# Finer steps for the decays that run between the tiles of v and the gate

## The chip, the cores and the metric

The kernel runs on 1 core of one Trainium2 chip. The metric is the device time of one execution in microseconds (us), median of several runs. All products are made in float32 precision from three products of split operands (high by high, high by low, low by high).

## The reference

One encoder block for 2048 tokens of width 1024. The first layer mixes a short convolution (512 channels) and a bidirectional gated linear attention of 4 heads (keys of 64, values of 128). Only the second part bears on the change:

```python
h = rms_norm(x, mix_norm)
z = h @ w_in                     # conv B, C, u; q, k, v, g; two low-rank gates
la_f = log_sigmoid(lr_f @ w_af + b_af) / 16      # decays, forward
la_b = log_sigmoid(lr_b @ w_ab + b_ab) / 16      # decays, backward
# per direction, in chunks: b = cumsum(la); q * exp(b), k * exp(-b),
# states carried over the chunks, o = (masked q k^T) v + q S
o = fwd + bwd - diag
y_gla = rms_norm(o, gla_norm) * silu(g)
x = x + concat([y_conv, y_gla]) @ w_out
# then cross-attention into 256 memory tokens, an MLP with squared ReLU, a final norm
```

## The kernel before, in words

The block is staged over the two halves of 1024 tokens. For each half, the operand of the norm is prepared, queries and keys are projected (`qk`), then the low-rank gates with the first half of the columns of g (`lr_g`), then the remaining columns of g and v (`vg`), and for the first half the convolution (`conv`). The weights come through `load_w` or `load_st`: a load into a `raw` buffer (L131 in `load_w`) and a split into a high part (a cast on ACT, L117) and a low part (a subtraction on DVE, L118). A product of split operands is `mm3`, L145 to L147.

`vg` works through three groups of columns, each 256 wide: one of g, two of v. In a group it makes eight token tiles of 128 x 256, each a chain of 24 matmuls into one of the four PS banks, so there are 24 tiles. `vg_store` evicts each: for g a Silu on ACT (L251), for v a copy on DVE (L249); then a store into the DRAM buffer zg or zv (L253). Behind each tile, `vg` takes one step of the generator `meanwhile`.

In the second half `meanwhile` is `decays()`, which makes the decays of heads 0 and 1 beside the tiles. For each head `gla_decay` has four steps of one small product with two evictions (L386 to L388), a step with two exponentials (L390), a step with two logarithms (L392), and then the part that the change touches, once for each half hf of the tokens:

- `sums(hf)`: on DVE a subtraction (L397), four running sums (L400), two small copies of the chunk's middle and end (L405, L406) and a subtraction (L407);
- `apply(hf)`: on ACT the exponentials for keys and queries (L411, L414); for keys and then queries, two blocks each: two DMAs from zk or zq on SP (L420) and a product on DVE (L422).

A last step makes the decay factors between chunks (L432 to L435). First come the four product steps of head 0, then those of head 1, then the rest of head 0, then the rest of head 1. Steps left over when the 24 tiles are done run behind them.

This stretch is in a block in which the instructions of PE, ACT and DVE keep the order in which they are written; the planner may put instructions from outside the block between them. The order on SP, which issues all DMAs, and on POOL, and everything behind the block, is laid out by the planner from its own estimates, and is then fixed.

Behind the block come the states of head 0: `gla_states`, with transposed keys (`keys`, L457, copied by ACT in L459), loads of v from zv (`load_v`, L440), products of the two (L465 in `upd`), their eviction (L469) and the `scan` over the chunks on DVE (L474). Then, head by head, `gla_out` (`attn` L485 to L489, `outp` L496 to L506, `fin` L512 to L515) beside the next head's states, and behind it the decays of head h + 2 through the same `gla_decay`, with no tile between its steps. The convolution of the second half (`conv(1, ...)`) is written behind all that, and the planner fills PE's waits with its products.

Of the kernel before, what the change touches and what calls it, by code (L numbers as in the profile page):

```python
# [30 lines left out]
def block_kernel(ctx, tc, x, mem, wm, wv, wlg, wlog, wout, wxk, wxv, wxqT, wxo, wup, wdn,  # L31
# [9 lines left out]
    def A4(dt=F32, shape=(P, 1024)):  # L41
        return big.tile(list(shape), dt, tag="a", name="a4", bufs=NA)

    def G4(dt=F32, shape=(P, 1024)):
        return big.tile(list(shape), dt, tag="g", name="g4", bufs=NG)
# [13 lines left out]
    def GT(dt=F32, shape=(P, 512)):  # L59
        return big.tile(list(shape), dt, tag="gt", name="gt", bufs=8)  # L60
# [4 lines left out]
    def GS(n, dt=F32):  # L65
        return big.tile([P, 16], dt, tag="gs", name="gs", bufs=9)[:, :n]
# [4 lines left out]
    def PG(shape=(P, 512)):  # L71
        return psp.tile(list(shape), F32, tag="pg", name="pg", bufs=4)
# [38 lines left out]
    def in_order(first, then):  # L111
        tc.add_manual_dep(then.ins, first.ins.name,
                          mybir.DependencyInfo(mybir.DependencyClass.NoSync, mybir.DependencyReason.DATA),
                          reason="one table set at a time")
# [28 lines left out]
    def mm3(ps, L, R, first, last):  # L143
        (lh, ll), (rh, rl) = L, R
        nc.tensor.matmul(ps, lh, rh, start=first, stop=False)  # L145
        nc.tensor.matmul(ps, lh, rl, start=False, stop=False)  # L146
        mark["pe"] = nc.tensor.matmul(ps, ll, rh, start=False, stop=last)  # L147
# [226 lines left out]
    def gla_decay(h, res):  # L374

        pr, r0 = h // 2, (h % 2) * 64
        hs = slice(h * P, (h + 1) * P)
        Q, K = [G4(), G4()], [G4(), G4()]
        pm, pe, de = GS(16), GS(16), GS(16)
        res.append((Q, K, de))  # L380

        for hf in range(2):
            for bi in range(2):
                ps = PG()
                sl = slice(bi * TB, (bi + 1) * TB)
                mm3(ps, (wlh[:, hs], wll[:, hs]), (lr[hf][0][:, sl], lr[hf][1][:, sl]), True, True)  # L386
                nc.scalar.activation(K[hf][:, sl], ps, AF.Abs)
                nc.vector.tensor_scalar_min(Q[hf][:, sl], ps, 0.0)  # L388
                yield
        exps = [nc.scalar.activation(K[hf], K[hf], AF.Exp, scale=-1.0) for hf in range(2)]  # L390
        yield
        lns = [nc.scalar.activation(K[hf], K[hf], AF.Ln, bias=1.0) for hf in range(2)]  # L392
        in_order(exps[1], lns[0])
        yield

        def sums(hf):
            nc.vector.tensor_tensor(out=K[hf], in0=Q[hf], in1=K[hf], op=ALU.subtract)  # L397
            for i in range(4):
                sl = slice(i * 256, (i + 1) * 256)
                nc.vector.tensor_tensor_scan(out=Q[hf][:, sl], data0=reset, data1=K[hf][:, sl], initial=0.0,  # L400
                                             op0=ALU.mult, op1=ALU.add)

            pv = Q[hf].rearrange("p (c t) -> p c t", t=P)
            m8 = pm[:, 8 * hf:8 * hf + 8].unsqueeze(2)
            nc.vector.tensor_copy(m8, pv[:, :, 63:64])  # L405
            nc.vector.tensor_copy(pe[:, 8 * hf:8 * hf + 8].unsqueeze(2), pv[:, :, 127:128])  # L406
            nc.vector.tensor_tensor(out=pv[:, :, 0:64], in0=pv[:, :, 0:64], in1=m8.broadcast_to([P, 8, 64]),  # L407
                                    op=ALU.subtract)

        def apply(hf):  # L410
            e = nc.scalar.activation(K[hf], Q[hf], AF.Exp, scale=nsgn)  # L411
            if hf == 0:
                in_order(lns[1], e)
            nc.scalar.activation(Q[hf], Q[hf], AF.Exp, scale=sgn)  # L414
            for T, z in ((K[hf], zk), (Q[hf], zq)):
                for bi in range(2):
                    r = GT()
                    c0 = hf * 1024 + bi * TB
                    for o in (0, 64):
                        nc.sync.dma_start(r[o:o + 64], z[pr][r0:r0 + 64, c0:c0 + TB])  # L420
                    sl = slice(bi * TB, (bi + 1) * TB)
                    nc.vector.tensor_tensor(out=T[:, sl], in0=T[:, sl], in1=r, op=ALU.mult)  # L422

        sums(0)
        yield
        apply(0)
        sums(1)
        yield
        apply(1)
        yield  # L430

        nc.vector.memset(de, 0.0)  # L432
        nc.vector.tensor_tensor(out=de[0:64, 1:16], in0=pe[0:64, 0:15], in1=pm[0:64, 1:16], op=ALU.add)
        nc.vector.tensor_tensor(out=de[64:128, 0:15], in0=pe[64:128, 0:15], in1=pm[64:128, 1:16], op=ALU.add)
        nc.scalar.activation(de, de, AF.Exp, scale=1.0 / 16.0)  # L435
        yield
# [396 lines left out]
    def decays():  # L833
        gens = [gla_decay(h, dec) for h in (0, 1)]
        for g in gens:
            for _ in range(4):
                next(g)
                yield
        for g in gens:
            for _ in g:  # L840
                yield
# [15 lines left out]
    for h in range(H):  # L857
        attn, outp, fin = gla_out(h, *dec[h][:2], St)
        if h + 1 < H:
            St, keys, upd, scan = gla_states(h + 1, *dec[h + 1])  # L860
        for j in range(6):
            if j < 4:
                attn(j)
                if h + 1 < H:
                    keys(j)
            if 0 < j < 5:
                outp(j - 1)
                if h + 1 < H:
                    upd(j - 1)
            if j > 1:  # L870
                fin(j - 2)
        if h + 1 < H:
            scan()
        if h + 2 < H:
            for _ in gla_decay(h + 2, dec):
                pass
# [362 lines left out]
    sums = [A4(F32, (P, 2, TB)) for _ in range(4)]  # L1239
# [172 lines left out]
```

## Time and profile before

| | |
|---|---|
| runs | 2677.62 us median of 3 (2676.23 to 2678.01) |
| profiled execution | 2673.82 us; its span, first to last instruction, 2672.0 us |
| mean granted clock of TensorE | 0.988 |
| PE, DVE, ACT, POOL busy | 97%, 61%, 35%, 10% of the span |
| the 24 tiles of the second half with their decays | about 482 to 564 us of the span |
| of them the 16 tiles of v | from 510.5 us on |
| linear attention and the convolution behind it | about 564 to 870 us |

The profile is of one execution. Times within it are us from the start of the span. PE is the matmul side of TensorE and PEld its weight loads, which overlap the matmuls; SPq is the queue in which SP issues DMAs. A row of a timeline gives start, length, engine, line, operation, what is written and read, shapes and count; in brackets stands how long the engine had been idle and what ended that. A row of waits gives who waited for whom, the total, the number and the longest. The chain of waits goes back from the last instruction to what released each step.

### The profile page before, as it was taken

The numbers are of one execution on the slowest core, as the hardware profiler recorded it, in microseconds if no ns is written. First come the engines' busy times: TensorE is split into PE (matmuls) and PEld (weight loads), VectorE is DVE, ScalarE is ACT, GpSimd is POOL, SyncE is SP. The second block draws the span as 40 slices with busy tenths as digits, with TensorE's granted clock in tenths as the row PEclk, the third lists the DMA queues.
The fourth block names the chain that finished last, engine by engine and source line by source line (L and its number), as shares of the span: only waits on it lengthen the run. The fifth ranks groups of instructions, "written<-read, shape, count | busy, mean of one in ns | idle before, by whom it ended". The sixth has DMA issues, their size and how long they took to land.

```text
span 2672.0 us, 34688 instructions
## 1 busy us (share of the span) xinstructions
PE 2580.3 (97%) x13560; PEld 2199.2 (82%) x13560; DVE 1627.1 (61%) x2502; ACT 934.0 (35%) x1432; POOL 259.9 (10%) x178
## 2 busy tenths in 40 slices
PE   7999999989989999999999999999999999999998
PEld 7898888877777787999997888788887888888887
DVE  6512364367766555444468566865555768788887
ACT  6411143334435443232225333443333323222322
POOL 0000000000000000000000000000002324243233
PEclk9999999999999999999999999999999999999999
DMA  7512355234445453110125333343328664555232
GB/s 258 179 60 67 107 175 174 74 91 127 123 117 171 146 181 111 46 50 33 64 79 185 115 107 114 111 161 111 122 99 309 229 196 156 179 162 183 95 116 106
DMA packets 198308, 353.26 MB, mean 132 GB/s; under 512 B 17344, under 2 KB 73792, under 8 KB 198144
## 3 DMA queue, kind: packets, MB, share of 16 engines
q1 hardware_dynamic: 198144, 351.05, 40.2%
q8 instruction: 106, 1.74, 0.3%
q14 instruction: 58, 0.48, 0.1%
HBM read 262.90 MB, written 88.08 MB: 131 GB/s over the span
## 4 chain that ended last, share of the span: by engine, by line
PE 79%; DVE 10%; DMA 5%; ACT 3%; issue 2%; POOL 1%; SPq 0%; DVEq 0%; POOLq 0%; ACTq 0%
PE ps L1016 12%; PE pg L1260 10%; PE ps L1260 10%; PE ps L145 9%; PE ps L147 9%; PE ps L146 9%; PE pg L1016 9%; PE pg L145 2%; PE pg L146 2%; PE pg L147 2%; DVE a L118 2%; DMA gt<-zv 1%; DVE st L474 1%; DMA raw<-zy 1%; DVE a L928 1%
## 5 line engine op out<-in xcount | busy, mean ns | idle before, releaser
L145 PE MATMUL ps<-a,a 128*128 128x512 f32 (+1 forms) x840 | 306.1, 364 | 6.4 <-DVE t L249 5.9
L146 PE MATMUL ps<-a,a 128*128 128x512 f32 (+1 forms) x840 | 306.0, 364 | 0.0
L147 PE MATMUL ps<-a,a 128*128 128x512 f32 (+1 forms) x840 | 305.0, 363 | 0.0
L1260 PE MATMUL pg<-a,g 128*128 128x512 f32 x1176 | 285.8, 389 | 3.6 <-DVE a L928 1.2
L1016 PE MATMUL ps<-a,g 128*128 128x512 f32 x1152 | 282.6, 390 | 2.5 <-DVE a L118 1.4
L1260 PE MATMUL ps<-a,g 128*128 128x512 f32 x1176 | 284.9, 389 | 0.0
L1016 PE MATMUL pg<-a,g 128*128 128x512 f32 x1152 | 278.4, 389 | 1.7 <-ACT g L117 1.1
L1260 PEld LDWEIGHTS pg<-a,g 128*128 128x128 f32 x1176 | 220.4, 188 | 51.3 <-ACT a L117 2.8
L1260 PEld LDWEIGHTS ps<-a,g 128*128 128x128 f32 x1176 | 220.7, 188 | 45.8
L1016 PEld LDWEIGHTS ps<-a,g 128*128 128x128 f32 x1152 | 215.9, 188 | 48.5 <-DVE a L118 2.1
L1016 PEld LDWEIGHTS pg<-a,g 128*128 128x128 f32 x1152 | 215.9, 188 | 48.1 <-ACT g L117 2.0
L117 ACT CAST a<-raw 128x1024 fp32r<-128x1024 f32 (+1 forms) x128 | 130.0, 1022 | 331.2 <-PE ps L1260 102.6
L118 DVE TENSOR_TENSOR a<-raw,a 128x1024 fp32r<-128x1024 f32 (+1 forms) x128 | 156.3, 1228 | 122.9 <-ACT a L117 121.1
L117 ACT CAST g<-gt 128x512 fp32r<-128x512 f32 x180 | 103.8, 618 | 334.8 <-PE pg L1016 192.8
L145 PEld LDWEIGHTS ps<-a,a 128*128 128x128 f32 x840 | 161.5, 192 | 32.6 <-DVE t L249 4.7
L147 PEld LDWEIGHTS ps<-a,a 128*128 128x128 f32 x840 | 161.8, 193 | 23.2
L146 PEld LDWEIGHTS ps<-a,a 128*128 128x128 f32 x840 | 161.8, 193 | 23.2 <-issue 0.2
L118 DVE TENSOR_TENSOR g<-gt,g 128x512 fp32r<-128x512 f32 x180 | 129.7, 758 | 49.1 <-ACT g L117 49.0
L928 DVE TENSOR_TENSOR t<-pg,t 128x512 f32<-128x512 f32 x64 | 44.2, 690 | 166.6 <-issue 127.9
L153 POOL TENSOR_TENSOR sm<-sm,nhalf 128x2 f32<-128x2 f32 (+1 forms) x26 | 24.3, 933 | 991.2 <-DVE sm L151 991.2
L118 DVE TENSOR_TENSOR g<-raw,g 128x1024 fp32r<-128x1024 f32 (+3 forms) x90 | 98.6, 1106 | 34.8 <-ACT g L117 34.6
L117 ACT CAST g<-raw 128x1024 fp32r<-128x1024 f32 (+3 forms) x90 | 85.4, 959 | 97.6 <-PE ps L146 17.7
(325 smaller groups left out, 5203.0 us busy)
## 6 DMA issues: line engine op xcount, KB each, us to landing
raw<-zu SPq DMA_DIRECT2D x64, 512.0 KB, 4.0
t<-in_wdn SPq DMA_DIRECT2D x84, 256.0 KB, 3.7
raw<-in_wm SPq DMA_DIRECT2D x32, 512.0 KB, 4.0
raw<-in_wup SPq DMA_DIRECT2D x32, 512.0 KB, 4.1
cv<-in_wup SPq DMA_DIRECT2D x32, 512.0 KB, 5.0
zu<-gt SPq DMA_DIRECT2D x64, 256.0 KB, 2.3
zu<-t SPq DMA_DIRECT2D x64, 256.0 KB, 3.9
cv<-zu SPq DMA_DIRECT2D x32, 512.0 KB, 5.1
```

The costliest lines, as they stand in the source:

```text
L117: mark["act"] = nc.scalar.copy(hi, src)
L118: nc.vector.tensor_tensor(out=lo, in0=src, in1=hi.bitcast(F32), op=ALU.subtract)
L145: nc.tensor.matmul(ps, lh, rh, start=first, stop=False)
L146: nc.tensor.matmul(ps, lh, rl, start=False, stop=False)
L147: mark["pe"] = nc.tensor.matmul(ps, ll, rh, start=False, stop=last)
L153: nc.gpsimd.tensor_tensor(out=r, in0=v, in1=nhalf[:, :n], op=ALU.pow)
L474: nc.vector.scalar_tensor_tensor(out=St[r, a], in0=St[r, b], scalar=de[r, a:a + 1], in1=St[r, a], op0=ALU.mult, op1=ALU.add)
L928: eng.tensor_tensor(out=out, in0=a, in1=b, op=op)
L1016: nc.tensor.matmul(ps, W[w][:, ks], X[x][kt], start=first and kt + w + x == 0, stop=kt == 3 and w == 1, skip_group_check=not first)
L1260: nc.tensor.matmul(ps, l, r, start=not chained and k == 0 and l is wh and r is x[k][0], stop=k == n - 1 and l is wl, skip_group_check=chained)
```

## The change

The steps are cut anew. apply() becomes a generator that yields behind the products of the keys and behind those of the queries, and each half's sums get a step of their own. The instructions and their order among the decays stay as they were; what stands between them, the evictions, is dealt out differently.

```diff
@@ in gla_decay, apply(hf) @@
                         nc.sync.dma_start(r[o:o + 64], z[pr][r0:r0 + 64, c0:c0 + TB])
                     sl = slice(bi * TB, (bi + 1) * TB)
                     nc.vector.tensor_tensor(out=T[:, sl], in0=T[:, sl], in1=r, op=ALU.mult)
-
-        sums(0)
-        yield
-        apply(0)
-        sums(1)
-        yield
-        apply(1)
-        yield
+                yield
+
+        for hf in range(2):
+            sums(hf)
+            yield
+            yield from apply(hf)
 
         nc.vector.memset(de, 0.0)
```

The `yield` in apply() stands in the loop over keys and queries, behind its two blocks.

## The prediction

> **What bounds the kernel now.** I read the page's busy times first, then its groups, then the chain of waits and the single engines' timelines around the groups that wait.
>
> ```profile
> PE 2580.3 (97%) x13560; PEld 2199.2 (82%) x13560; DVE 1627.1 (61%) x2502; ACT 934.0 (35%) x1432; POOL 259.9 (10%) x178
> L145 PE MATMUL ps<-a,a 128*128 128x512 f32 (+1 forms) x840 | 306.1, 364 | 6.4 <-DVE t L249 5.9
> ```
>
> PE is busy for 97% of the span, so a gain has to come from PE's waits. The second row shows 6.4 us of idle PE ahead of a group of matmuls, of which 5.9 until the eviction of v (L249) on DVE. A tile of v needs a bank of the four PS banks, so tile k cannot start before the eviction of tile k-4. The chain of waits says what the eviction was behind:
>
> ```profile
> 543.49 1.24 DVE g L397
> ...
> 553.00 2.45 DVE g L400 x4
> ...
> 556.29 0.43 DVE t L249
> 556.76 0.58 PE ps L145
> ...
> 565.36 0.43 DVE t L249
> ...
> 566.33 5.47 DMA gt<-zv
> ...
> 571.94 1.13 PE pg L465 x8
> ```
>
> The chain runs through head 1's decays on DVE, then through one eviction (556.29) into PE, through the last eviction (565.36) and its store into the queue of SP, and through the load of v into the first states' product (L465). The weight loads of PE show the waits and, between them, the pace of the tiles (start, duration, idle before):
>
> ```profile
> 510.51 0.19 PEld L145 LDWEIGHTS ps<-st,a 128*128 128x128 f32 x1 [0.36 <-ACT t L251]
> 533.93 0.19 PEld L145 LDWEIGHTS ps<-a,a 128*128 128x128 f32 x1 [1.57 <-issue]
> 537.58 0.19 PEld L145 LDWEIGHTS ps<-a,a 128*128 128x128 f32 x1 [0.72 <-DVE gs L432]
> 556.76 0.29 PEld L145 LDWEIGHTS ps<-a,a 128*128 128x128 f32 x1 [4.72 <-DVE t L249]
> 563.97 0.46 PEld L457 LDWEIGHTS pg<-cst,g 128*128 128x128 f32 x4
> 571.91 0.97 PEld L465 LDWEIGHTS pg<-gt 128*128 128x128 f32 x8 [1.95 <-issue]
> ```
>
> I count tiles and steps 0 to 23. Tile 8 (the first of v) starts at 510.51, tile 16 at 533.93, tile 17 at 537.58, tile 22 at 556.76; the transposes of the keys (L457) follow tile 23. Tiles 8 to 15 take (533.93 - 1.57 - 510.51)/8 = 2.73 us each, tiles 17 to 21 (556.76 - 4.72 - 537.58)/5 = 2.89. The three waits are 1.57 + 0.72 + 4.72 = 7.01 us. After the longest there is a second loss, in the windows (length, PE, PEld, DVE, ACT, POOL busy, granted clock, DMA share, GB/s):
>
> ```profile
> 556.76:564.07 7.31, 7.31 (x49) 7.31 (x49) 5.50 (x12) 3.21 (x4) 0.00 (x0) 0.77 0.27 90
> 564.07:571.94 7.87, 6.32 (x34) 5.04 (x32) 1.56 (x2) 2.02 (x3) 0.00 (x0) 1.00 0.83 243
> 564.00:870.00 306.00, 274.95 (x1542) 225.14 (x1542) 212.38 (x425) 123.83 (x176) 21.53 (x32) 0.97 0.43 128
> ```
>
> Tiles 22 and 23 took 7.31 us at a clock of 0.77 where two tiles take 5.78: 1.53 us. All that the evictions cost PE here is 7.01 + 1.53 = 8.54 us.
>
> **The change, part by part.** No instruction is added, removed or resized. apply() yields behind each product (keys, queries) and sums() is a step of its own, so a head's last part goes from 6 steps to 9, and both heads from 2 x 10 = 20 steps to 2 x 13 = 26. There are 24 tiles, so two steps (head 1's last query product and its decay factors) come behind the last eviction. Heads 2 and 3 run through the same generator with no tile in between, in the same order as before: nothing.
>
> What a step costs on DVE and ACT:
>
> ```profile
> 525.14 0.42 DVE L249 COPY t<-ps 128x256 f32<-128x256 f32 x1
> 526.44 2.50 DVE L422 TENSOR_TENSOR g<-g,gt 128x512 f32<-128x512 f32 x4 [0.89 <-ACT g L411]
> 537.47 1.20 DVE L118 TENSOR_TENSOR st<-raw,st 128x1024 fp32r<-128x1024 f32 x1
> 551.75 1.22 DVE L397 TENSOR_TENSOR g<-g,g 128x1024 f32<-128x1024 f32 x1
> 557.59 2.50 DVE L422 TENSOR_TENSOR g<-g,gt 128x512 f32<-128x512 f32 x4 [0.88 <-ACT g L411]
> 560.37 0.07 DVE L432 MEMSET gs<- 128x16 f32 x1
> 560.86 1.08 DVE L249 COPY t<-ps 128x256 f32<-128x256 f32 x3
> 562.71 1.22 DVE L118 TENSOR_TENSOR a<-raw,a 128x1024 fp32r<-128x1024 f32 x1 [0.76 <-PE ps L146]
> 564.22 1.23 DVE L118 TENSOR_TENSOR a<-raw,a 128x1024 fp32r<-128x1024 f32 x1 [0.29 <-PE ps L146]
> ```
> ```profile
> 539.09 1.99 ACT L390 ACTIVATE g<-g 128x1024 f32<-128x1024 f32 x2
> 542.39 2.01 ACT L392 ACTIVATE g<-g 128x1024 f32<-128x1024 f32 x2
> 556.40 1.15 ACT L411 ACTIVATE g<-g,cst 128x1024 f32<-128x1024 f32 x1 [5.92 <-DVE g L407]
> 557.59 1.15 ACT L414 ACTIVATE g<-g,cst 128x1024 f32<-128x1024 f32 x1
> ```
>
> A sums() is 556.29 - 551.75 = 4.54 us, a pair of products 2.50/2 = 1.25, an eviction 0.36 to the next start (three of them 1.08), an exponential 1.15, the decay factors' three small instructions 560.86 - 560.37 = 0.5. The old fused step is products, then sums, with no eviction between them: at 556.29 an eviction comes out whose tile had long ended. In the new order no eviction has more than one sums() or one pair of products between it and the eviction before it.
>
> The new order on DVE, at these prices. Head 0's first sums end at 525.14 as now. Then: eviction 11 to 525.50; keys from 526.44 (the exponential) to 527.69; eviction 12 to 528.05; queries to 529.30; eviction 13 to 529.66; second sums to 534.20; eviction 14 to 534.56; keys from 535.45 to 536.70; eviction 15 to 537.06; queries to 538.31; eviction 16 to 538.67. Undelayed, tile 16 starts at 532.36 and each next one 2.89 later, so tile 18 needs eviction 14 by 538.14 (there 3.6 us early) and tile 20 needs eviction 16 by 543.92 (5.2 early). The factors, with the weight split of 1.20 that stood there before, end at about 540.2, and head 1's exponentials start at 540.3, 1.2 later than the 539.09 of now; its first logarithm is done at 543.49 + 1.2 = 544.7. Eviction 19 waits for tile 19's end (543.92), which is less. Sums to 549.2, eviction 20, keys from 550.5 to 551.8, eviction 21, queries to 553.4, eviction 22 to 553.8, sums to 558.3, eviction 23. Tile 23 starts at 552.59 undelayed and needs eviction 19 alone. So no tile waits, PE's 7.01 us of waits go, and with them the cold stretch: tile 23 ends at about 555.5, not 564.07, 8.54 us earlier.
>
> What is late next: eviction 23, 2.8 us behind its tile. Behind it in SP's queue stands its store, and behind that the load of v for the first states:
>
> ```profile
> 563.96 1.84 SPq L131 DMA_DIRECT2D raw<-in_wm  x2
> 565.90 0.38 SPq L253 DMA_DIRECT2D zv<-t  x1
> 566.33 15.31 SPq L440 DMA_DIRECT2D gt<-zv  x5
> ```
>
> Store at 558.8 (565.36 to 565.90 now: 0.54 behind the start of the eviction), load at 559.2 and not 566.33, landing 5.47 later, L465 at 564.8 and not 571.94: 7.1 us earlier. PE covers part of the wait as now, with 6.3 us of transposes and convolution products (564.07 to 571.91 less 1.95 is 5.9 by the weight loads, 6.32 by the matmuls), from 555.5 to 561.8, and would stand for 3.0 us where it stood 1.95. The two steps behind the last tile, two exponentials and 1.25 + 1.25 + 0.5 us on DVE, end at about 563.0, ahead of L465's end at 565.9, where DVE is wanted next: nothing. The zk and zq loads (eight on SP for each head) have buffers free from head 0's last queries on, 538.3, as now: nothing.
>
> The one cost that the trace does not show is where two weight splits (L118, 1.23 each, free to start when tile 23's halves are done) fall. Ahead of eviction 23 they make the load 2.46 later: gain 7.1 - 2.5 = 4.6. At the other end the load goes ahead of the two 512 KB weight loads that shared the DMA engines with it (share 0.83 in the window from 564.07) and PE's wait goes too: 8.54 + 1.95 = 10.5. I take 7.1, because now those splits start when PE releases their buffers and DVE has no gap before eviction 23.
>
> After that the shift has to live through the rest of the linear-attention stage: from 564 to 870 PE is idle 306.00 - 274.95 = 31 us, in waits for states and loads that hang on this chain, and from 870 on it is nearly full. I let the 7.1 pass through.
>
> **Sum.** The profiled execution took 2673.82 us (span 2672.0, 1.8 around it): 2673.8 - 7.1 = 2666.7. It lies 3.8 below the median of the runs, 2677.62, so in the terms of the median 2670.5.
>
> **A rule against it.** How long may PE stand before the clock drops? These windows are 2 us long; PE is the first pair, then the clock:
>
> ```profile
> 572.00:574.00 2.00, 2.00 (x15) 1.00 0.59 156
> 590.00:592.00 2.00, 0.68 (x4) 1.00 0.00 0
> 592.00:594.00 2.00, 0.09 (x1) 1.00 0.00 0
> 594.00:596.00 2.00, 2.00 (x11) 0.55 0.00 0
> ```
> ```profile
> PE pg L496 <- DVE st L474: 4.4, 1, 4.4
> ```
>
> The wait of 1.95 us left the clock at 1.00, that before 594 (2.00 - 0.68 + 2.00 - 0.09 = 3.2 us) brought 0.55. The new wait of 3.0 us at L465 lies between the two. If it drops the clock, 1.53 us are lost and the gain is 5.6. [...]
>
> **Rivals.** First, the gain is mostly hidden: the splits go ahead of eviction 23, PE stands 5.5 us at L465 and runs cold: 7.1 - 2.5 - 1.5 = 3.1, or 2674.5. For it: DVE is nearly full there and now both splits do stand ahead of the eviction. Against it: today they are there because DVE was ahead of PE. Chance 0.28, between no gain and 5.4.
>
> Second, slower: the fixed order behind the last tile is drawn up anew, convolution products are spent on the longer wait at L465, and are lacking at the scans of the states (L474), where PE stood 4.4 us at its longest by the row above (the list of waits between 780 and 870). The price of one such wait with a cold stretch is 4.4 + 1.5 = 5.9. On all three heads that follow it is 17.8 - 7.1 = 10.7 slower, 2688.3; it is slower by over the bound below from 7.1 + 5.4 = 12.5 us of added waits on, a little over two. For it: 31 us of waits show how little cover there is. Against it: the products are the same ones and their number too. Chance 0.16.
>
> **How the numbers follow.** 0.2% (5.4 us) is about what a measurement of this kernel can tell from no change. The forecast's own range is 5.4 to 10.5 us gained, 2667.1 to 2672.2, chance 0.56; hidden 0.28; slower 0.16. So faster 0.56, same 0.28, slower 0.16. The range reaches down to the full gain with one scan's wait gone as well (10.5 + 4.4: 2662.7) and up to the hidden case with one scan's wait added (3.1 - 4.4: 2678.9).
>
> **What would show it.** PE shows no wait for L249 between 510 and 556; the transposes of the keys start near 555.5; the clock stays 1.00 up to there; the last eviction lies some 2.8 us behind its tile; L465 starts near 564.8; the idle time of the 306 us behind that stays near 31. It is wrong if the last eviction comes after 561 (splits ahead), if L465 starts later than 567, or if the waits at L496 and L497 grow by what was won.

## The result and the profile after

The changed kernel takes 2656.41 us (median of 4 runs, 2653.76 to 2658.7) against 2676.93 us before (4 runs, 2674.5 to 2678.01). The ratio is 0.9928, 95% interval 0.9914 to 0.9941: 19.3 us faster. Forecast were 7.1, and 2656.41 lies below the range. The profiled execution of the changed kernel took 2657.17 us, its span is 2655.4. In it all lines behind the change have numbers smaller by two: L463 is what was L465, L472 what was L474.

The first group of matmuls on the page of the changed kernel no longer has a wait ahead of it:

```profile
L145 PE MATMUL ps<-a,a 128*128 128x512 f32 (+1 forms) x840 | 304.2, 362 | 0.0
```

I cut the part of the span that the change can touch into four stretches: the 16 tiles of v (from tile 8 to the first transpose of keys, L457), from there to the first product of the states (L465), from there to the first eviction of the output projection (L919; linear attention and convolution), and the output projection up to its last block's evictions (L907). The windows have length, busy time of PE, PEld, DVE, ACT, POOL, granted clock, DMA share and GB/s. Before:

```profile
510.50:564.10 53.60, 47.17 (x386) 46.58 (x386) 40.78 (x77) 30.35 (x30) 0.00 (x0) 0.97 0.38 118
564.10:571.90 7.80, 6.28 (x33) 4.98 (x31) 1.56 (x2) 2.02 (x3) 0.00 (x0) 1.00 0.83 243
571.90:847.60 275.70, 247.55 (x1419) 203.57 (x1420) 195.21 (x395) 105.35 (x150) 21.53 (x32) 0.96 0.41 124
847.60:1021.90 174.30, 169.03 (x719) 135.89 (x717) 88.60 (x137) 78.45 (x110) 0.00 (x0) 0.98 0.47 155
```

After:

```profile
509.90:554.80 44.90, 44.90 (x386) 44.90 (x386) 34.23 (x63) 27.84 (x27) 0.00 (x0) 1.00 0.47 141
554.80:559.90 5.10, 4.23 (x24) 3.33 (x23) 5.08 (x10) 2.34 (x4) 0.00 (x0) 1.00 0.55 166
559.90:832.50 272.60, 247.42 (x1424) 203.75 (x1424) 197.62 (x402) 108.08 (x154) 20.61 (x32) 0.97 0.43 129
832.50:1002.30 169.80, 166.73 (x723) 135.11 (x722) 88.40 (x137) 77.80 (x109) 0.00 (x0) 1.00 0.48 158
```

In the tiles PE is now busy for the whole window at clock 1.00: 53.6 - 44.9 = 8.7 us. That is close to the forecast's 8.54. But every later stretch is shorter too: 2.7, 3.1 and 4.5 us, 10.3 together, where the forecast had a loss of 1.4 in the second and nothing in the others. Some of the 2.7 is only moved: 24 matmuls (4.23 us) now stand ahead of L463 where 33 (6.28 us) stood ahead of L465, and the other nine run later. Over all four stretches the same 2557 matmuls keep PE busy for 463.3 us and not 470.0, and PE's idle time falls from 41.4 to 29.1 us: of the 19.0 us, 6.7 are products that run faster and 12.3 are waits. Two places show the later gain. SP's queue in the changed kernel (L438 is the load of v):

```profile
555.30 0.33 SPq L131 DMA_DIRECT2D raw<-in_wm  x1
555.68 0.79 SPq L438 DMA_DIRECT2D gt<-zv  x1
558.76 0.33 SPq L131 DMA_DIRECT2D raw<-in_wm  x1
559.90 0.32 SPq L253 DMA_DIRECT2D zv<-t  x1
```

The first load of v stands ahead of the last store of v, by 4.2 us; before it stood behind. And on PE, in the output projection, a wait of the kernel before has no counterpart after:

```profile
904.64 0.66 PE L627 MATMUL pg<-t,oneb 128*128 128x512 f32 x1 [2.92 <-DVE t L118]
```

So the order of what is written behind the block was laid out anew. Compared instruction by instruction (the instructions there are the same in both programs), the two orders differ in 990 of 9880 places on PE, 273 of 2162 on DVE, 103 of 1078 on ACT, 72 of 804 on SP and in none on POOL.

### The profile page after: what moved, and what is told of

Same layout as the page of the kernel before. It is cut to its first block, busy times and chain, and to the rows that moved or that the text cites. A ratio compares the mean times of both kernels' runs of the same rounds, so it can differ in the third digit from the quotient of the medians.

```text
span 2655.4 us, 34702 instructions
## 1 busy us (share of the span) xinstructions
PE 2574.6 (97%) x13560; PEld 2196.0 (83%) x13560; DVE 1629.3 (61%) x2502; ACT 933.3 (35%) x1432; POOL 255.5 (10%) x178
## 4 chain that ended last, share of the span: by engine, by line
PE 78%; DVE 10%; DMA 5%; ACT 3%; issue 3%; POOL 1%; SPq 0%; DVEq 0%; POOLq 0%; ACTq 0%
PE ps L1014 12%; PE ps L1258 10%; PE pg L1258 10%; PE ps L145 9%; PE ps L147 9%; PE ps L146 9%; PE pg L1014 9%; PE pg L145 2%; PE pg L147 2%; PE pg L146 2%; DVE a L118 2%; DMA gt<-zv 2%; DVE st L472 1%; ACT a L117 1%; DVE a L926 1%
```

## The experiments

My theory after the result: the change has two effects that add up, the finer steps themselves (8.5 us, as forecast) and a new order behind the block, of which the place of the first load of v is one part. Rival 1: it is all the steps, and the new order only follows them. Rival 2: it is all the new order.

To tell these apart, one kernel has the steps of one version and the order of the other. At the end of the program each instruction written behind the block is tied, on its engine, to issue after the one ahead of it in a recorded order. That adds no wait between engines other than those that the data need:

```diff
+    by = {i.name: i for i in nc.cur_bb.bb.instructions}
+    for engine, ids in ORDER.items():          # recorded from the other version
+        for first, then in zip(ids, ids[1:]):
+            tc.add_manual_dep(by[f"I-{then}"], by[f"I-{first}"].name,
+                              mybir.DependencyInfo(mybir.DependencyClass.NoSync, mybir.DependencyReason.DATA),
+                              reason="pinned order")
```

Instructions of the block itself, the stores of v among them, are placed between these by the planner.

**Old steps, new order.**

> The old steps of the decays, with every instruction written behind the block (on PE, DVE, ACT, SP and POOL) held in the order that the changed kernel's planner gave it. Theory (two sources: the waits of the tiles, 8.5 us, and the order that was laid out anew behind the block): the three waits for the evictions of v and the cold stretch stay (7.0 + 1.5 us), the first load of v goes out ahead of the last store, and the rest of the stage runs as after: 8 to 11 us below before, 2666 to 2669. Rival 1 (the steps alone; the new order only follows them): as before, 2674 to 2680. Rival 2 (the new order alone): as after, about 2657.

Measured: 2668.76 us, ratio 0.9968 (0.9956 to 0.9981). Its four stretches:

```profile
507.60:562.30 54.70, 48.24 (x386) 47.67 (x386) 40.89 (x77) 30.34 (x30) 0.00 (x0) 0.94 0.36 116
562.30:568.00 5.70, 4.22 (x23) 3.28 (x21) 1.56 (x2) 2.02 (x3) 0.00 (x0) 1.00 0.73 228
568.00:840.60 272.60, 246.86 (x1424) 203.68 (x1424) 195.02 (x395) 105.98 (x150) 20.60 (x32) 0.97 0.42 127
840.60:1012.80 172.20, 168.61 (x723) 136.16 (x722) 88.57 (x137) 78.02 (x110) 0.00 (x0) 0.99 0.48 156
```

The waits in the tiles are all there (54.7), and the three stretches behind are 2.1, 3.1 and 2.1 us shorter than before. The new order alone is worth about 8.6 us by the ratio (5 to 12 by its interval) and 6.2 by the stretches. Both rivals fall.

**New steps, old order.**

> The new steps, with every instruction written behind the block held in the order of the kernel before. Theory: no waits for the evictions, tile 23 ends some 8.5 us earlier, the last store and behind it the first load of v some 5 to 7 us earlier; 6 to 9 us below before, 2668 to 2671. Rival 1: as after, about 2657. Rival 2: as before, 2674 to 2680.

Measured: 2668.62 us, ratio 0.9969 (0.9956 to 0.9981).

```profile
512.60:557.50 44.90, 44.90 (x386) 44.90 (x386) 34.25 (x63) 27.82 (x27) 0.00 (x0) 1.00 0.47 142
557.50:566.70 9.20, 6.28 (x33) 4.99 (x32) 7.92 (x17) 4.54 (x6) 0.00 (x0) 1.00 0.60 181
566.70:845.50 278.80, 249.40 (x1419) 205.55 (x1420) 195.21 (x396) 105.74 (x150) 21.49 (x32) 0.96 0.41 123
845.50:1017.80 172.30, 167.38 (x719) 135.27 (x717) 88.59 (x138) 78.00 (x110) 0.00 (x0) 0.99 0.47 156
```

This is the kernel that I had forecast. 8.7 us are won in the tiles, 1.4 given back before L465 (so 7.3 earlier there; the forecast had 7.1), 3.1 given back in linear attention and 2.0 won in the output projection, so 6.2 are left; by the ratio it is 8.3.

That 7.3 meets 7.1 so closely is in part luck, as the rows around the last eviction of v show:

```profile
562.14 0.42 DVE L249 COPY t<-ps 128x256 f32<-128x256 f32 x1
562.59 0.33 SPq L253 DMA_DIRECT2D zv<-t  x1
562.97 3.37 SPq L438 DMA_DIRECT2D gt<-zv  x4
```

This execution enters the stage 2.1 us later than that of the kernel before (485.0 against 482.9 at L387), so the eviction comes at 560.0 in the old count and the load goes out at 560.9, both 1.7 later than forecast (558.3 and 559.2). The load made up for it: its product starts 3.75 us behind the issue (566.72), where the forecast took 5.6 from the kernel before (566.33 to 571.94).

**One DMA moved, in both directions.** Only the first load of v changes its place in SP's queue:

```diff
 # changed kernel, its order held; the load behind the weight load and the last store
-weight load, LOAD OF V, weight load, last store of v
+weight load, weight load, last store of v, LOAD OF V
 # kernel before, its order held
-weight load, weight load, last store of v, LOAD OF V
+weight load, LOAD OF V, last store of v, weight load
```

> The changed kernel with its whole order held, but for one DMA: the first load of v goes out behind the last store of v and the weight load ahead of it, as before. Theory: L465 starts about 4 us later than in the changed kernel (the store goes out at 559.9, the load at 555.7), and most of that stays: 2659 to 2661. Rival: PE has other work there and the load was hidden: 2655 to 2658.

Measured: 2665.34 us, ratio 0.9951 (0.9937 to 0.9965), some 6 us above the changed kernel by the ratios (0.9951 - 0.9928), more than I expected. The timeline's row of L463 says why (in brackets the wait ahead of it). In the changed kernel:

```profile
559.90 1.13 PE L463 MATMUL pg<-gt 128*128 128x128 f32 x8 [0.87 <-DMA gt<-zv]
```

And with the load behind the store:

```profile
563.92 2.05 PE L463 MATMUL pg<-gt 128*128 128x128 f32 x8 [5.02 <-ACT gs L433]
```

The wait grows by 4.15 us, and behind a wait of 5 us the eight products take 2.05 us and not 1.13: the granted clock has dropped (0.90 over the window from 554.6 to 563.9, 1.00 in the tiles), and that costs on top. (The profile names ACT as what came last; ACT's copies of the keys were done by 556.4, and the load was issued at 560.15.)

> The kernel before with its whole order held, but for the same DMA, moved the other way: the first load of v ahead of the last store and of the second weight load. Theory: the load goes out at about 564.3 and not 566.3 and meets less traffic, L465 starts 2 to 4 us earlier, the total falls by 1 to 4: 2673 to 2676. Rival (the place of this load is the larger part of the unexpected gain): 8 us or more below before, under 2669.

Measured: 2672.71 us, ratio 0.9982 (0.9973 to 0.9991): 4.8 us for one DMA, with an interval of 2.4 to 7.2 and a little more than the 1 to 4 expected. The DMA passed a weight load as well as the store, so this is not the price of the store alone. The second stretch falls from 7.8 to 6.2, less than the 2 to 4 expected, and the two behind it by 1.1 and 1.5; why those fall was not followed.

**New steps, old order, but the load ahead.** The same move in the kernel with new steps and the old order:

> The new steps with the old order, and of the new order only the place of the first load of v (ahead of the last store and of the second weight load). Theory (three sources that add up: steps, place of the load, rest of the order): 3 to 6 us below the new steps with the old order (2668.6), 2663 to 2666, and still 6 to 10 above the changed kernel. Rival (the load's place is all that the new order has to give): 2655 to 2659.

Measured: 2667.61 us, ratio 0.9952 (0.9937 to 0.9967). Its stretches are 44.9, 6.2, 276.7 and 172.6 us. Against the new steps with the old order (505.2 in all) the sum of 500.4 is 4.8 lower; the ratios differ by 0.0017, 4.6 us, with intervals that overlap. The median lies above the 2663 to 2666 expected: the six runs spread from 2659.79 to 2669.0, and the profiled one, 2660.09, is among the fastest. Against the changed kernel (492.4) 8.0 are still missing, 4.1 in linear attention and 2.8 in the output projection, 1.1 ahead of L465. By these single executions the load's place is not all that the new order gives; by the ratios the difference is 6.4 us (0.9952 - 0.9928), and the two intervals just overlap.

**The load still earlier.** In the changed kernel the load goes out still further ahead. I counted two stores and a weight load; in the run it passes one store (553.08) and one weight load (555.34) and is issued at 552.14. The second weight load (560.36) comes behind the last store there:

> The changed kernel with its order held, but the first load of v goes out two stores and a weight load earlier (about 552 to 553 instead of 555.7). Theory: the 0.87 us that PE stood at L463 goes, and little else is to be had there: 0 to 2 us below the changed kernel, 2654 to 2657. Rival (the place of this load sets the whole chain behind it): L463 starts as much earlier as the load, 3 us: 2652 to 2654.

Measured: 2659.73 us, ratio 0.9940 (0.9925 to 0.9955), above both ranges. L463 starts 1.0 us earlier and does not wait, but the next L463 waits for its own load:

```profile
565.43 1.28 PE L463 MATMUL pg<-gt 128*128 128x128 f32 x8 [2.26 <-DMA gt<-zv]
```

Nothing is won: the stretches are 44.9, 4.1, 274.6 and 169.8, 493.4 in all.

**Half of the change, each half alone,** with the order that the planner then gives:

```diff
 # sums alone, against the kernel before (apply without a yield inside, as there)
-sums(0)
-yield
-apply(0)
-sums(1)
-yield
-apply(1)
-yield
+for hf in range(2):
+    sums(hf)
+    yield
+    apply(hf)
+    yield
```

```diff
 # products alone, against the changed kernel
-for hf in range(2):
-    sums(hf)
-    yield
-    yield from apply(hf)
+sums(0)
+yield
+first = apply(0)
+next(first)         # products of the keys
+yield
+next(first)         # products of the queries, and the second half's sums with them
+sums(1)
+yield
+yield from apply(1)
```

> Half of the change: each half's sums are a step of their own, the products of keys and queries stay together (22 steps). Theory: the evictions come just in time (19 at about 552.3, needed at 552.6), so PE waits under 1 us for them; the last eviction comes near 562 and the load of v behind the last store near 562.5, L465 at 566 to 567: 2663 to 2669. Rival (any cut that frees PE gives the whole gain): 2654 to 2659.

> The other half: steps end behind each product, the second half's sums stay with the first half's query product (24 steps). Theory: no wait for an eviction (a step of at most 5.8 us on DVE), the load of v goes out ahead of the last store, near 560: L465 at 564 to 566, 2660 to 2667, by the order laid out anew. Rival (any cut that frees PE gives the whole gain): 2654 to 2659.

Measured: 2668.91 us, ratio 0.9964 (0.9951 to 0.9977), and 2669.43 us, ratio 0.9965 (0.9953 to 0.9978). The tiles take 45.0 and 44.9 us: either half alone frees PE. Against the changed kernel 12.2 and 11.4 us of the four stretches are missing. The sums alone lose 8.1 of them ahead of the first product of the states, the products alone 3.2; the rows of that product in the two kernels:

```profile
571.22 2.05 PE L463 MATMUL pg<-gt 128*128 128x128 f32 x8 [6.86 <-DMA gt<-zv]
```
```profile
565.51 2.04 PE L468 MATMUL pg<-gt 128*128 128x128 f32 x8 [4.52 <-DMA gt<-zv]
```

For the sums alone 2668.91 lies at the upper edge of what I had put (2663 to 2669). Its profiled execution enters the stage 2.5 us later than that of the kernel before (485.4 against 482.9), so L463 at 571.22 is 568.7 in the old count, later than the 566 to 567 expected, and the load of v, issued at 566.29, went out at 563.8 in that count, 1.3 later than expected. For the products alone L468 comes about where I had put it (565.51, entered 1.8 later, so 563.7, against 564 to 566), but the stretch behind it took 280.9 us, longer than in any other kernel here, and the time missed the estimate of 2660 to 2667. Of the 8.3 us by which that stretch is longer than in the changed kernel, 6.3 are slower products (1426 keep PE busy for 253.7 us, 1424 for 247.4, at a mean clock of 0.95 against 0.97); what brings the clock down was not followed further. Both times lie above the rival's 2654 to 2659, so freeing PE in the tiles is not the whole gain.

**Other new orders.** Is the changed kernel's order a lucky draw? The new steps, with the orders that the planner gave these two halves:

> The new steps with everything behind the block held in the order that the planner gave the kernel with the sums alone. The two new orders differ in 277 places of PE. Theory (what the new orders share, the later convolution products and no wait in the output projection, is the gain): 2655 to 2661, like the changed kernel. Rival (the changed kernel's order was a lucky draw): 2664 to 2670, like the new steps with the old order.

> The new steps with everything behind the block held in the order that the planner gave the kernel with the products alone; in it the first load of v goes out ahead of the weight load too. Theory: 2655 to 2661. Rival: 2664 to 2670.

Measured: 2660.49 us, ratio 0.9946 (0.9933 to 0.9959), and 2660.06 us, ratio 0.9945 (0.9931 to 0.9958). All stretches in one table, in us, from the profiled executions:

| steps | order | load of v | tiles | to L465 | attention, convolution | output projection | sum | ratio |
|---|---|---|---|---|---|---|---|---|
| old | old | behind | 53.6 | 7.8 | 275.7 | 174.3 | 511.4 | 1 |
| old | old | ahead | 53.4 | 6.2 | 274.6 | 172.8 | 507.0 | 0.9982 |
| old | new | ahead | 54.7 | 5.7 | 272.6 | 172.2 | 505.2 | 0.9968 |
| new | old | behind | 44.9 | 9.2 | 278.8 | 172.3 | 505.2 | 0.9969 |
| new | old | ahead | 44.9 | 6.2 | 276.7 | 172.6 | 500.4 | 0.9952 |
| new | new | behind | 44.8 | 9.3 | 275.4 | 169.0 | 498.5 | 0.9951 |
| new | new | ahead | 44.9 | 5.1 | 272.6 | 169.8 | 492.4 | 0.9928 |
| new | new | further ahead | 44.9 | 4.1 | 274.6 | 169.8 | 493.4 | 0.9940 |
| new | of sums alone | ahead | 44.9 | 5.0 | 274.8 | 168.7 | 493.4 | 0.9946 |
| new | of products alone | further ahead | 44.9 | 3.6 | 278.1 | 167.7 | 494.3 | 0.9945 |
| sums alone | its own | behind | 45.0 | 13.2 | 276.3 | 170.1 | 504.6 | 0.9964 |
| products alone | its own | ahead | 44.9 | 8.3 | 280.9 | 169.7 | 503.8 | 0.9965 |

Each kernel was profiled once, so how far its stretches scatter is not known. Outside the four stretches all programs run the same instructions in the same order, and there the twelve executions differ by up to 8.3 us (span less sum, 2157.9 to 2166.2; up to the first stretch, 507.6 to 513.0). So differences of a few us in the table are no more than hints.

With the new steps, the new orders that have the load ahead, or further ahead, end at 492.4 to 494.3, the old order at 500.4: 6 to 8 us, a good part of it in the output projection (167.7 to 169.8 against 172.6). The ratios, which take in all runs, say less: 0.9928 to 0.9946 for the four kernels with a new order, 0.9952 (0.9937 to 0.9967) for the old one with the load ahead, 2 to 6 us apart with intervals that overlap. The two medians lie within the range expected, but the kernel before ran at 2675.8 beside them; at 0.9945 to 0.9946 they would be 2662 to 2663 beside its 2676.93, between the theory and the rival. So it is not settled whether the changed kernel's order was a lucky draw: two other orders keep most of its gain, and its own lead over them, some 5 us by the ratios, may be luck. No version is clearly faster than the changed kernel.

## Why the prediction went wrong

**The bound and its price: right.** PE's waits for evictions and the cold stretch behind them (a clock of 0.77) were put at 8.54 us; the tiles take 8.7 less. Either half of the change alone does that too (45.0 and 44.9 us).

**The order on DVE: right to a few tenths, but for the last eviction.** The changed kernel enters the stage 0.6 us earlier, so its times are to be read 0.6 later. DVE's timeline:

```profile
527.01 0.42 DVE L249 COPY t<-ps 128x256 f32<-128x256 f32 x1
533.42 0.42 DVE L249 COPY t<-ps 128x256 f32<-128x256 f32 x1
...
552.92 1.22 DVE L397 TENSOR_TENSOR g<-g,g 128x1024 f32<-128x1024 f32 x1
554.05 1.22 DVE L118 TENSOR_TENSOR a<-raw,a 128x1024 fp32r<-128x1024 f32 x1
555.18 2.43 DVE L400 TENSOR_TENSOR_SCAN g<-cst,g 128x256 f32<-128x256 f32 x4
557.53 1.20 DVE L118 TENSOR_TENSOR a<-raw,a 128x1024 fp32r<-128x1024 f32 x1
559.46 0.42 DVE L249 COPY t<-ps 128x256 f32<-128x256 f32 x1
```

Evictions 12 and 14 were put at 527.69 and 534.20 and come at 527.6 and 534.0 in the old count. The last was put at 558.3 and comes at 560.1: the two weight splits (554.05, 557.53) did fall ahead of it, among the instructions of the last sums, which I held for the less likely end. By the forecast that should have lowered the gain to 4.6. It did not: in the changed kernel the load no longer waits for that eviction, and with the old order held the load came 1.9 us sooner behind its issue, as shown above.

**The step that failed: "Behind it in SP's queue stands its store, and behind that the load of v".** That holds for the old order only. In the new one the load goes out at 555.68, ahead of the store at 559.90, so the late eviction delays nobody; L463 starts 12.0 us earlier than before (11.4 with the entry taken off) and not 7.1. I had priced a better place of this load, but as a swap with weight loads behind the store, and as an end of the range.

**The term that was missing: the new order behind the block.** The forecast let the 7.1 "pass through" and knew a new order only as the second rival, as a loss: convolution products spent early, waits at the scans. It is a gain here. By the ratios, times 2677 us: steps 8.3 (old order held), place of the load 4.6 more, the rest of the order 6.4 more, 19.3 together; in the profiled stretches 6.2, 4.8 and 8.0, 19.0 together. The intervals of the single kernels are some 3.5 us to each side, so a difference of two is good to some 5 us: that the steps and the new order each bring a gain is shown (8.3 and 8.6 us, each alone), the split of the order's part is not. In the stretches the new order was worth 505.2 - 492.4 = 12.8 with the new steps and 6.2 with the old, as if the two helped each other; by the ratios it is 11.0 and 8.6, which does not show it. One reason for it can be read off: with the old steps the new order sends the load out at 562.53 (entered 2.9 us earlier, so 565.4 in the old count), only 0.9 earlier than before (566.33), with the new steps at 555.68 (556.3), 10 earlier.

**Rivals.** The first (hidden: a wait of 5.5 us at L465, run cold) did not come in the changed kernel, but it is what either half alone shows (6.86 and 4.52 us at L463, then 2.05 us for eight products). The second was right that the order is drawn up anew, and wrong on what it does: the new order spends fewer matmuls ahead of L465, 24 and not 33, and the longest wait at the scans shrinks (rows below).

**The clock.** The forecast left open whether a wait of 3.0 us at L465 costs the clock, yet its sum counted no such cost. That any wait of this length leaves the clock as it was is an estimate of mine that no run shows: the forecast's rows had 1.95 us with a clock of 1.00 behind it and 3.2 us with 0.55, and the runs gave both outcomes near 3 us. With the new steps and the old order PE waits 2.94 there, as forecast, and the eight products behind it take 1.13 us, as in the changed kernel; behind 4.52, 5.02 and 6.86 us they take 2.04 to 2.05.

```profile
566.72 1.13 PE L463 MATMUL pg<-gt 128*128 128x128 f32 x8 [2.94 <-ACT gs L433]
```

But the length of a wait does not decide it alone. The wait of 3.2 us ahead of 594 in the forecast's windows was followed by a clock of 0.55. Here it is in the kernel before, and below it the same wait in the changed kernel with the load still earlier (L494 and L495 there):

```profile
593.91 0.49 PE L496 MATMUL pg<-st,g 128*128 128x128 f32 x2 [3.23 <-DVE st L474]
594.21 0.62 PE L497 MATMUL pg<-gt 128*128 128x128 f32 x2
...
584.91 0.46 PE L494 MATMUL pg<-st,g 128*128 128x128 f32 x2 [3.22 <-DVE st L472]
585.21 0.39 PE L495 MATMUL pg<-gt 128*128 128x128 f32 x2
```

The first went cold (two products at L497 take 0.62 us) and the second did not (0.39 us for two at L495). And in the kernel before, the 2.92 us at L627 were followed by a clock of 0.74 between 900 and 910 us, though 2.94 us elsewhere were not. So these rows give no bound between warm and cold, and that the 2.94 us at L465 cost nothing may be luck. Nor is a wait of about 3 us safe, though the forecast's sum took it to be: 2.92 and 3.23 us cost the clock here (it was 0.74 and 0.55 behind them).

**Left open.** Which of the 990 other places on PE, or which of DVE, ACT and SP, bring the rest of the gain was not tried one by one. Two waits of PE separate the orders in all twelve profiles. At the scan of the last head it stands 4.4 us in the four kernels with the old order and 2.4 to 2.5 in the other eight; before, and in the changed kernel:

```profile
795.79 0.76 PE L496 MATMUL pg<-st,g 128*128 128x128 f32 x2 [4.38 <-DVE st L474]
...
773.18 0.46 PE L494 MATMUL pg<-st,g 128*128 128x128 f32 x2 [2.43 <-DVE st L472]
```

At L627 (L625 in the changed kernel) its longest wait is 2.1 to 2.9 us in the old orders and 0.4 to 0.5 in the others. Other waits grow: the longest at the transposes of the keys is 1.9 us before and 3.5 after. So these two do not add up to the gain, and with the old steps and the new order the output projection still took 172.2. No run holds a kernel's own order and changes nothing, so what the ties themselves cost is not measured either.

## What to carry to other kernels

When only a part of a program has a fixed order and a planner lays out the rest, a change inside the fixed part is two changes; hold the order of the rest and measure each by itself, and give the new order a price of both signs, here as large as the change (8.6 and 8.3 us). When a wait of PE on an eviction goes, look at what stands in the DMA queue behind the last eviction: a load that needs nothing from a store should not be queued behind it (4.8 us, 2.4 to 7.2, for one DMA that passed a store and a weight load). A step that keeps an engine busy for long can be cut in more than one way: either half of this cut freed PE in the tiles as well as the whole, and they differed in what came late behind them.

## What was not expected of the hardware

The same instructions take the kernel to this stage at different times: the first small product's eviction (L387) lies at 480.0 us of the span in one profiled execution and at 485.4 in another, with nothing changed ahead of it. Differences of a few us between single executions are to be read within a stage, or from many runs. And a wait costs more than its length when the clock drops with it: 4.15 us of added wait at L463 came with 0.92 us more for its eight products alone. Waits of 2.92 and 3.23 us were followed by such a drop (a clock of 0.74 and 0.55) and waits of 2.94 and 3.22 us were not (1.13 us for eight products, 0.39 for two), so near 3 us a forecast should price the drop as a chance.
